# Modulation sums of the opening stage moved from VectorE to TensorE, with the last two blocks loaded singly

## Chip, cores and metric

The kernel runs on one core of a Trainium2 chip. The metric is device time in microseconds, the median of several runs.

## The reference, cut to what matters

One encoder layer on 2048 frames of width 1024. The conditioning vector `c` (1024 values) gives three vectors, and the first two modulate the input before the big projection:

```python
mod = c @ w_ada[l] + b_ada[l]                    # (1024) @ (1024 x 3072)
shift, scale, gate = jnp.split(mod, 3, axis=-1)
h = x * (1.0 + scale[:, None, :]) + shift[:, None, :]
proj = h @ w_in[l]                               # 1024 -> 3584, seven groups of 512
```

The seven groups of the projection feed a gated mixer and a stick-breaking attention; both results are multiplied by gates, projected out, scaled by `1 + gate`, added to the residual and normalised. All is float32. The kernel keeps that precision by splitting each operand of the big products into a rounded high part and a low remainder, and by summing three products (high by high, low by high, high by low).

## The kernel before, in words

The 2048 frames are four chunks of 512; the width of 1024 is eight blocks of 128. The kernel opens with chunk 3. For each of the eight blocks b it needs the shift and scale of these 128 columns (two columns of `w_ada`, 1024 rows each), the transposed input block, and the weights of the k and v groups (`w_in`). The output of a block is the modulated, transposed input in a high and a low half (`hts[b]`), and six accumulators in PSUM (`accs`: four of k, two of v) take three matmuls each from every block, 18 matmuls of 512 columns per block, 144 in all. This stage (lines 393 to 473) is called the opening here.

The order of TensorE, SyncE (which starts the loads), VectorE and ScalarE in the opening is the order in which the lines are written. A list `parts` (line 421) cuts the eight blocks into groups: 0; 1; 2 and 3; 4 and 5; 6 and 7. For each group:

- `load_ada` (line 283) loads the two slices of `w_ada`, for the shift and the scale, in tiles of 128 rows by partition; a group of one block takes two tiles with four DMAs, a group of two blocks four tiles with eight DMAs. Eight tiles of this kind exist, so a load waits for the release of an earlier group's tiles.
- `modulation` (line 296) multiplies on VectorE each of the eight row blocks by its part of `c` and adds it to `macc` (lines 302 and 304): eight instructions, over shift and scale together, 256 columns for one block and 512 for two.
- `modulation_sum` (line 307) sums `macc` over its 128 partitions on TensorE: for each block and each of shift and scale one float32 matmul with `macc` as the stationary operand and one column of ones as the moving one (line 312). Each such matmul is two instructions in the trace.
- `modulation_put` (line 316) adds `b_ada` and puts the sums into `mod_t` (line 319).
- `turn_x` (line 265) transposes a block of the input with four matmuls (line 268); `hidden` (line 271) applies the shift and scale on ScalarE (line 273); a ScalarE copy rounds that to the high half (line 454), and VectorE subtracts for the low half (line 461).
- `quarter` (line 116) loads raw weights of k and v for two blocks, into three buffers; `high` (line 416) rounds them on ScalarE, `low` (line 419) subtracts, on VectorE for k and on GpSimd for v.

`main(n)` issues n entries of the list `pending`, each the three matmuls of one block and one accumulator (line 160). After a group's transpose and sums comes `main(1)`; at the end of the group `main(len(pending))` issues what was left of the groups before, the new group's entries are appended, and `main(len(pending) - 6)` leaves the last block of them for the next group. So the products of block 0 stand behind the sums of block 1, the products of block 1 behind the sums of blocks 2 and 3, and so on. `advance` issues the VectorE steps of the next group's `modulation` between other VectorE work.

After the opening the results of k and v are stored, and the next stage (line 482 on) starts with the remaining products of chunk 3 and the modulation of chunk 2; its input loads (line 475) are queued on SyncE behind those of the opening.

Of the kernel before, what the change touches and what calls it, by code (L numbers as in the profile page):

```python
# [12 lines left out]
ALU = mybir.AluOpType  # L13
# [3 lines left out]
P = 128  # L17
D = 1024
S = 2048
NB = D // P  # L20
# [15 lines left out]
def layer_kernel(ctx: ExitStack, tc: tile.TileContext, x, c, w_ada, b_ada, w_in, ln_v_g, ln_v_b,  # L36
                 w_spatial, b_spatial, w_out, ln_g, ln_b, out):
    nc = tc.nc
# [40 lines left out]
    ones = const.tile([P, P], F32, name="ones")  # L79
# [26 lines left out]
    def pj(nm, shape=(P, 512)):  # L106
        return ps.tile(list(shape), F32, tag="pj", bufs=2, name=nm)

    def tr(nm, shape=(P, 512)):
        return ps.tile(list(shape), F32, tag="tr", bufs=3, name=nm)  # L110

    def zt(nm):
        return ps.tile([P, 2, CH], F32, tag="z", bufs=1, name=nm)


    def quarter(ws, g, b2, nm):

        raw = raw4(f"raw_{nm}_{b2}")
        nc.sync.dma_start(raw, w_in[b2 * 256:(b2 + 1) * 256, g * 512:(g + 1) * 512]
                          .rearrange("(b p) n -> p b n", p=P))  # L120
        sl = slice(2 * (b2 % 2), 2 * (b2 % 2) + 2)
        return raw, ws[b2 // 2][0][:, sl, :], ws[b2 // 2][1][:, sl, :]
# [27 lines left out]
    def mm3(acc, hts, ws, b, m, chan):  # L150

        sl = slice(m * P, (m + 1) * P)
        wh, wl = ws[b // 4][0][:, b % 4, :], ws[b // 4][1][:, b % 4, :]
        hh, hl = hts[b][:, 0, :], hts[b][:, 1, :]
        if chan:
            trip = ((wh[:, sl], hh), (wl[:, sl], hh), (wh[:, sl], hl))
        else:
            trip = ((hh[:, sl], wh), (hh[:, sl], wl), (hl[:, sl], wh))
        for i, (l_, r_) in enumerate(trip):
            nc.tensor.matmul(acc, l_, r_, start=(b == 0 and i == 0), stop=(b == NB - 1 and i == 2))  # L160
# [80 lines left out]
    with ExitStack() as sa:  # L241
        pa = sa.enter_context(tc.tile_pool(name="pa", bufs=1))

        def p2(nm, dt=F32):
            return pa.tile([P, CH], dt, tag="t2a", bufs=8, name=nm)
# [7 lines left out]
        c_t, bada_t = cb_t[:, 0:NB], cb_t[:, NB:3 * NB]  # L253
# [5 lines left out]
        def load_x(ci, b2):  # L259
            xt = pa.tile([P, 4, 256], F32, tag="xt", bufs=4, name=f"xt_{ci}_{b2}")  # L260
            nc.sync.dma_start(xt, x[ci * CH:(ci + 1) * CH, b2 * 256:(b2 + 1) * 256]
                              .rearrange("(t p) n -> p t n", p=P))
            return xt

        def turn_x(ci, b, xt):
            tp = tr(f"xT_{ci}_{b}")
            for t in range(4):
                nc.tensor.transpose(tp[:, t * P:(t + 1) * P], xt[:, t, (b % 2) * P:(b % 2 + 1) * P], ident)  # L268
            return tp
# [13 lines left out]
        def load_ada(b0, nb):  # L283

            rows = 4 // nb
            wts = []
            for r in range(NB // rows):
                wt = hta(f"wada_{b0}_{r}", (P, rows, 2, nb * P), F32)
                for i in range(2):
                    nc.sync.dma_start(wt[:, :, i, :], w_ada[r * rows * P:(r + 1) * rows * P,  # L290
                                                            i * D + b0 * P:i * D + (b0 + nb) * P]
                                      .rearrange("(b p) n -> p b n", p=P))
                wts += [wt[:, i] for i in range(rows)]
            return wts

        def modulation(b0, nb, wts):

            macc = p2(f"macc_{b0}")[:, 0:2 * nb * P].rearrange("p (two n) -> p two n", two=2)
            yield macc
            for b, wt in enumerate(wts):  # L300
                if b == 0:
                    nc.vector.tensor_scalar(macc, wt, c_t[:, b:b + 1], None, op0=ALU.mult)
                else:
                    nc.vector.scalar_tensor_tensor(macc, wt, c_t[:, b:b + 1], macc, op0=ALU.mult, op1=ALU.add)
                yield

        def modulation_sum(b0, nb, macc):

            mod_ps = ps.tile([P, 2 * nb], F32, tag="tr", bufs=3, name=f"mod_ps_{b0}")
            for i in range(2):  # L310
                for j in range(nb):
                    nc.tensor.matmul(mod_ps[:, i * nb + j:i * nb + j + 1], macc[:, i, j * P:(j + 1) * P],
                                     ones[:, 0:1], start=True, stop=True)
            return mod_ps

        def modulation_put(b0, nb, mod_ps):
            for i in range(2):
                cs = slice(i * NB + b0, i * NB + b0 + nb)
                nc.vector.scalar_tensor_tensor(mod_t[:, cs], mod_ps[:, i * nb:(i + 1) * nb], float(i), bada_t[:, cs],
                                               op0=ALU.add, op1=ALU.add)  # L320
# [74 lines left out]
        with tc.manual_schedule(engines={ET.PE, ET.SP, ET.DVE, ET.Activation}):  # L395
            zacc = zt("acc0")
            accs = [(pj("pk_0_0"), w_k, 0, True), (pj("pk_0_1"), w_k, 1, True), (tr("pk_0_2"), w_k, 2, True),
                    (ps.tile([P, 512], F32, tag="pv", bufs=1, name="pk_0_3"), w_k, 3, True),
                    (zacc[:, 0, :], w_v, 3, False), (zacc[:, 1, :], w_v, 2, False)]
            hts = []  # L400

            pending = []

            def main(n):
                for b, (acc, ws, m, chan) in pending[0:n]:
                    mm3(acc, hts, ws, b, m, chan)
                del pending[0:n]

            def advance(k=None):
                while k is None or k > 0:  # L410
                    if next(msteps, 0) == 0:
                        return
                    k = None if k is None else k - 1

            def high(raw, hi, lo):
                nc.scalar.copy(hi, raw)

            def low(raw, hi, lo, eng):
                eng.tensor_tensor(lo, raw, hi.bitcast(F32), op=ALU.subtract)

            parts = ((0, 1), (1, 1), (2, 2), (4, 2), (6, 2))
            xts = []
            wts = load_ada(*parts[0])
            xts.append(load_x(NC - 1, 0))
            rk = quarter(w_k, G_K, 0, "k")
            rv = None
            msteps = modulation(*parts[0], wts)
            macc = next(msteps)
            advance()
            for n, (b0, nb) in enumerate(parts):  # L430
                tps = [turn_x(NC - 1, b0, xts[b0 // 2])]
                mod_ps = modulation_sum(b0, nb, macc)
                main(1)
                fresh = b0 % 2 == 0
                rk0 = rk
                if n < len(parts) - 1:
                    b1, nb1 = parts[n + 1]
                    wts = load_ada(b1, nb1)
                    if n == 0:
                        rv = quarter(w_v, G_VB, 0, "v")  # L440
                    msteps = modulation(b1, nb1, wts)
                    macc = next(msteps)
                rv0 = rv
                if fresh:
                    high(*rk0)
                modulation_put(b0, nb, mod_ps)
                if nb == 2:
                    tps.append(turn_x(NC - 1, b0 + 1, xts[b0 // 2]))
                if fresh:
                    low(*rk0, nc.vector)  # L450
                hs = []
                for i in range(nb):
                    hs.append(hidden(NC - 1, b0 + i, tps[i]))
                    nc.scalar.copy(hs[i][1][:, 0, :], hs[i][0])
                if fresh:
                    high(*rv0)
                    low(*rv0, nc.gpsimd)
                advance(3)
                for i in range(nb):
                    hf, ht = hs[i]  # L460
                    nc.vector.tensor_tensor(ht[:, 1, :], hf, ht[:, 0, :].bitcast(F32), op=ALU.subtract)
                    hts.append(ht)
                    if i < nb - 1:
                        advance(1)
                if n < len(parts) - 1 and b1 % 2 == 0:
                    xts.append(load_x(NC - 1, b1 // 2))
                    rk = quarter(w_k, G_K, b1 // 2, "k")
                    rv = quarter(w_v, G_VB, b1 // 2, "v")
                advance()
                main(len(pending))  # L470
                pending += [(b, a) for b in range(b0, b0 + nb) for a in accs]
                main(len(pending) - 6)
            main(len(pending))
        with tc.manual_schedule(engines={ET.PE, ET.SP, ET.DVE, ET.Activation}):
            xnext = [load_x(NC - 2, b2) for b2 in range(NB // 2)]
# [440 lines left out]
    n = len(units)  # L916
# [4 lines left out]
    with tc.manual_schedule(engines={ET.PE}):  # L921
        for i in range(n + 3):
# [7 lines left out]
            f = load[i] * rate[phase[0]] * scale / 3 if i else 6000  # L930
# [42 lines left out]
```

## Time and profile before

| | us |
|---|---|
| median of 3 runs | 1317.86 (1316.92 to 1319.66) |
| the profiled execution | 1317.15 |
| its span | 1315.0 |
| TensorE busy | 1246.9 (95%) |
| VectorE busy | 950.8 (72%) |
| ScalarE busy | 556.3 (42%) |
| GpSimd busy | 212.4 (16%) |
| mean granted TensorE clock | 0.987 |

A row of the timeline has the start in microseconds from the span's start, the time that its instructions took, the engine (PE is TensorE's matmul, PEld its weight load, DVE VectorE, ACT ScalarE, POOL GpSimd, SPq the queue of SyncE), the line, the operation, output and inputs, and how many instructions were merged. In brackets stands the idle time before it and what ended it. Starts of consecutive matmuls tell their pace; the durations of matmuls overlap. A row of the windows gives busy microseconds and instruction counts by engine, the granted clock (1.00 is 2.4 GHz, 0.50 is 1.2 GHz), the mean busy share of the DMA engines and GB/s.

### The profile page before, as it was taken

To read this page: it belongs to the slowest core of one execution; us is meant where nothing else is said; L and a number is where in the kernel's file an instruction comes from. 1 tells how busy PE (TensorE), PEld (TensorE's weight loads), DVE (VectorE), ACT (ScalarE), POOL (GpSimd) and SP (SyncE) were. 2 spreads that over 40 slices of the span, in tenths; PEclk is the share of its full clock that TensorE was granted. 3 is DMA by queue.
4 is the path that set the end of the run, shared out by engine and by line. 5 is a ranking of instruction groups with operands and counts; after the bars stand their busy time and mean duration, and the time that the engine had idled before them with its cause. 6 is when DMAs were issued, how large, how long until landed. Compare 5 with 4: busy or idle time off the path is not lost.

```text
span 1315.0 us, 18685 instructions
## 1 busy us (share of the span) xinstructions
PE 1246.9 (95%) x6678; PEld 1055.5 (80%) x6678; DVE 950.8 (72%) x1358; ACT 556.3 (42%) x1063; POOL 212.4 (16%) x342
## 2 busy tenths in 40 slices
PE   4999999899889999899979999999999999999997
PEld 4788877688678888787868888888888888888875
DVE  6634453317678778888888887878788798888874
ACT  3333222214434454555555554545444444444430
POOL 1244333001110002233260000000000011010001
PEclk9999999899899999999989999999999999999999
DMA  9699886858789874674546483745759776754431
GB/s 318 202 365 326 281 276 198 280 176 263 254 267 312 245 224 144 207 226 141 156 115 188 114 252 98 236 111 158 213 174 282 224 207 161 201 167 149 128 101 48
DMA packets 202012, 269.20 MB, mean 205 GB/s; under 512 B 14880, under 2 KB 131648, under 8 KB 200896
## 3 DMA queue, kind: packets, MB, share of 16 engines
q1 hardware_dynamic: 191280, 234.41, 58.8%
q0 software_dynamic: 10592, 33.59, 7.5%
q8 instruction: 53, 0.87, 0.3%
q14 instruction: 39, 0.32, 0.1%
q10 hardware_dynamic: 48, 0.01, 0.0%
HBM read 180.37 MB, written 83.36 MB: 201 GB/s over the span
## 4 chain that ended last, share of the span: by engine, by line
PE 72%; issue 8%; DVE 8%; DMA 5%; POOL 3%; ACT 1%; SPq 1%; POOLq 0%; DVEq 0%; ACTq 0%
PE puz_False L160 13%; PE po L671 12%; PE pkv L160 11%; PE pqz_True L160 8%; PE tr L808 7%; PE pv L827 4%; PE z L778 4%; PE z L779 4%; PE pv L825 4%; PE pva_False L160 3%; DVE kp L793 2%; DMA wada<-in_w_ada_dram 2%; DMA qt<-q_d 1%; DVE wtl L68 1%; PE xT L268 1%
## 5 line engine op out<-in xcount | busy, mean ns | idle before, releaser
L793 DVE TENSOR_TENSOR_SCAN kp<-kp,kp,zero 128x512 f32<-128x512 f32 x192 | 241.5, 1286 | 48.8 <-ACT kp L782 48.6
L65 ACT CAST wth<-tr 128x512 fp32r<-128x512 f32 (+2 forms) x352 | 169.9, 487 | 249.0 <-PE tr L808 149.3
L68 DVE TENSOR_TENSOR wtl<-tr,wth 128x512 fp32r<-128x512 f32 (+2 forms) x352 | 194.1, 561 | 31.1 <-ACT wth L65 28.3
L671 PE MATMUL po<-wo,mt 128*128 128x512 f32 x744 | 201.9, 403 | 0.1
L782 ACT ACTIVATE kp<-z 128x128 f32<-128x128 f32 (+3 forms) x224 | 147.8, 691 | 101.6 <-PE z L779 99.9
L808 PE MATMUL tr<-ident,kp 128*128 128x128 f32 x1088 | 168.4, 275 | 6.6 <-DVE wtl L68 3.6
L785 POOL TENSOR_SCALAR_AFFINE_SELECT kp<-kp 128x128 f32<-128x128 f32 x128 | 56.5, 450 | 678.4 <-ACT kp L782 572.1
L671 PEld LDWEIGHTS po<-wo,mt 128*128 128x128 f32 x744 | 132.6, 188 | 24.2 <-DVE xr L681 0.5
L808 PEld LDWEIGHTS tr<-ident,kp 128*128 128x128 f32 x1088 | 128.4, 141 | 24.4 <-DVE wtl L68 3.4
L825 PE MATMUL pv<-wth,vs 128*128 128x256 f32 x576 | 143.1, 279 | 2.3 <-DVE ot L841 2.1
L827 PE MATMUL pv<-wtl,vs 128*128 128x256 f32 x576 | 142.4, 285 | 2.0 <-DVE wtl L68 2.0
L793 DVE TENSOR_TENSOR_SCAN kp<-kp,zero 128x128 f32<-128x128 f32 (+3 forms) x128 | 107.7, 865 | 34.6 <-POOL kp L785 32.0
L778 PE MATMUL z<-ks,qt 128*128 128x512 f32 (+2 forms) x320 | 115.7, 367 | 5.0 <-DMA qt<-q_d 4.3
L825 PEld LDWEIGHTS pv<-wth,vs 128*128 128x128 f32 x576 | 110.9, 193 | 11.0 <-DVE ot L841 4.3
L827 PEld LDWEIGHTS pv<-wtl,vs 128*128 128x128 f32 x576 | 110.9, 193 | 8.8 <-DVE wtl L68 2.4
L779 PE MATMUL z<-ks,qt 128*128 128x512 f32 (+2 forms) x320 | 116.7, 365 | 0.0
L160 PE MATMUL pkv<-wh_v,hta 128*128 128x512 f32 x224 | 75.8, 402 | 0.5 <-DVE el_k L68 0.5
L160 PE MATMUL pqz_True<-ht_qz,wh_q 128*128 128x512 f32 x192 | 70.0, 411 | 5.7 <-DMA ht_qz<-ht_d 5.7
L160 PE MATMUL puz_False<-wh_u,ht_uz 128*128 128x512 f32 x192 | 73.5, 411 | 1.7 <-DMA ht_uz<-ht_d 1.7
L778 PEld LDWEIGHTS z<-ks,qt 128*128 128x128 f32 x320 | 60.2, 188 | 17.6 <-ACT woh L65 4.7
L160 PE MATMUL pva_False<-wh_va,ht_va 128*128 128x512 f32 x192 | 71.8, 411 | 1.0 <-DMA ht_va<-ht_d 1.0
L160 PE MATMUL puz_False<-wh_za,ht_uz 128*128 128x512 f32 x192 | 72.6, 411 | 0.0
(191 smaller groups left out, 2234.5 us busy)
## 6 DMA issues: line engine op xcount, KB each, us to landing
ks<-k_d SPq DMA_DIRECT2D x160, 128.0 KB, 3.9
vs<-v_d SPq DMA_DIRECT2D x80, 256.0 KB, 3.6
qt<-q_d SPq DMA_DIRECT2D x64, 256.0 KB, 5.0
ht_d<-hta POOLq DMA_DIRECT2D x24, 512.0 KB, 5.8
ht_qz<-ht_d SPq DMA_DIRECT2D x24, 512.0 KB, 7.1
ht_va<-ht_d SPq DMA_DIRECT2D x24, 512.0 KB, 6.1
ht_uz<-ht_d SPq DMA_DIRECT2D x24, 512.0 KB, 5.9
wada<-in_w_ada_dram SPq DMA_DIRECT2D x32, 256.0 KB, 6.6
```

The source lines that it names most:

```text
L65: nc.scalar.copy(hi, src)
L68: (sub or nc.vector).tensor_tensor(lo, src, hi.bitcast(F32), op=ALU.subtract)
L160: nc.tensor.matmul(acc, l_, r_, start=(b == 0 and i == 0), stop=(b == NB - 1 and i == 2))
L671: nc.tensor.matmul(acc, ms[l_], w[:, r_, :], start=(b == 0 and i == 0), stop=(b == NB - 1 and i == 2))
L778: nc.tensor.matmul(z[:, j, 0:w_], hd.q[:, 0, qs], hd.k[self.s][:, 0:w_], start=True, stop=False)
L779: nc.tensor.matmul(z[:, j, 0:w_], hd.q[:, 1, qs], hd.k[self.s][:, 0:w_], start=False, stop=True)
L782: nc.scalar.activation(self.kp[:, js, 0:w_], z[:, js, 0:w_], AF.Sigmoid, scale=-ZSC)
L785: nc.gpsimd.affine_select(own, own, pattern=[[-1, P]], compare_op=ALU.is_gt, fill=1.0, base=0, channel_multiplier=1)
L793: nc.vector.tensor_tensor_scan(kp[:, j, 0:w_][:, ::-1], kp[:, j, 0:w_][:, ::-1], zero.broadcast_to([P, w_]), 1.0 if self.diag else self.pr ...
L808: nc.tensor.transpose(tp[:, e, j * P:(j + 1) * P], self.kp[:, j, kb * P:(kb + 1) * P], ident)
L825: nc.tensor.matmul(self.pv[:, cs], hd.v[self.s][:, kb, :], self.wt[0][:, kb, cs], start=self.diag and kb == 0, stop=False)
L827: nc.tensor.matmul(self.pv[:, cs], hd.v[self.s][:, kb, :], self.wt[1][:, kb, cs], start=False, stop=self.s == 0 and kb == self.nkb - 1)
```

## The change

The list of groups becomes 0; 1; 2 and 3; 4 and 5; 6; 7. For a group of one block (0, 1, 6, 7) VectorE does no modulation at all: TensorE sums shift and scale directly, with each of the eight 128 by 128 pieces of `w_ada` as the stationary operand and one column of `c` as the moving one, eight accumulating matmuls for each sum. For a group of two blocks VectorE sums only the scale (256 columns instead of 512), TensorE sums the shift directly. The low part of the v weights moves from GpSimd to VectorE, behind the low halves of the group. The products of block 0 and of block 1 are issued at the end of their own group, ahead of the next group's transpose and sums.

```diff
         def modulation(b0, nb, wts):
-            macc = p2(f"macc_{b0}")[:, 0:2 * nb * P].rearrange("p (two n) -> p two n", two=2)
+            if nb == 1:
+                yield None
+                return
+            macc = p2(f"macc_{b0}")[:, 0:nb * P]
             yield macc
             for b, wt in enumerate(wts):
                 if b == 0:
-                    nc.vector.tensor_scalar(macc, wt, c_t[:, b:b + 1], None, op0=ALU.mult)
+                    nc.vector.tensor_scalar(macc, wt[:, 1], c_t[:, b:b + 1], None, op0=ALU.mult)
                 else:
-                    nc.vector.scalar_tensor_tensor(macc, wt, c_t[:, b:b + 1], macc, op0=ALU.mult, op1=ALU.add)
+                    nc.vector.scalar_tensor_tensor(macc, wt[:, 1], c_t[:, b:b + 1], macc, op0=ALU.mult, op1=ALU.add)
                 yield
 
-        def modulation_sum(b0, nb, macc):
+        def modulation_sum(b0, nb, macc, wts):
             mod_ps = ps.tile([P, 2 * nb], F32, tag="tr", bufs=3, name=f"mod_ps_{b0}")
             for i in range(2):
                 for j in range(nb):
-                    nc.tensor.matmul(mod_ps[:, i * nb + j:i * nb + j + 1], macc[:, i, j * P:(j + 1) * P],
-                                     ones[:, 0:1], start=True, stop=True)
+                    col, cs = mod_ps[:, i * nb + j:i * nb + j + 1], slice(j * P, (j + 1) * P)
+                    if i and macc is not None:
+                        nc.tensor.matmul(col, macc[:, cs], ones[:, 0:1], start=True, stop=True)
+                        continue
+                    for b, wt in enumerate(wts):
+                        nc.tensor.matmul(col, wt[:, i, cs], c_t[:, b:b + 1], start=b == 0, stop=b == NB - 1)
             return mod_ps
...
-            parts = ((0, 1), (1, 1), (2, 2), (4, 2), (6, 2))
+            parts = ((0, 1), (1, 1), (2, 2), (4, 2), (6, 1), (7, 1))
...
-                mod_ps = modulation_sum(b0, nb, macc)
+                mod_ps = modulation_sum(b0, nb, macc, wts)
...
                 if fresh:
                     high(*rv0)
-                    low(*rv0, nc.gpsimd)
                 advance(3)
...
+                if fresh:
+                    low(*rv0, nc.vector)
                 if n < len(parts) - 1 and b1 % 2 == 0:
                     xts.append(load_x(NC - 1, b1 // 2))
...
                 pending += [(b, a) for b in range(b0, b0 + nb) for a in accs]
-                main(len(pending) - 6)
+                main(len(pending) - (6 if n > 1 else 0))
             main(len(pending))
```

## Rows read from the trace of the kernel before

**Rows 1.** Windows of ten microseconds: PE, PEld, DVE, ACT, POOL busy, clock, DMA share, GB/s

```profile
10.00:20.00 10.00, 2.62 (x13) 2.22 (x12) 7.58 (x12) 3.39 (x4) 2.38 (x1) 1.00 1.12 336
20.00:30.00 10.00, 10.00 (x43) 8.26 (x44) 7.94 (x15) 3.64 (x5) 0.00 (x0) 1.00 1.09 359
30.00:40.00 10.00, 8.61 (x45) 7.10 (x44) 8.70 (x10) 3.52 (x5) 2.73 (x1) 1.00 1.09 359
40.00:50.00 10.00, 9.27 (x45) 7.46 (x44) 9.74 (x13) 4.71 (x6) 2.73 (x1) 1.00 1.01 329
...
60.00:70.00 10.00, 10.00 (x50) 8.30 (x49) 3.26 (x6) 4.36 (x8) 5.38 (x10) 1.00 0.48 170
```

**Rows 2.** Timeline of TensorE, start to the first products

```profile
9.49 1.11 PE L268 MATMUL xT<-ident,xt 128*128 128x128 f32 x4 [5.16 <-DMA xt<-in_x_dram]
10.40 0.85 PE L312 MATMUL mod_ps<-ones,macc 128*128 128x1 f32 x4
11.11 1.09 PE L268 MATMUL xT<-ident,xt 128*128 128x128 f32 x4
19.59 1.01 PE L312 MATMUL mod_ps<-ones,macc 128*128 128x1 f32 x4 [7.38 <-DVE macc L304]
20.46 0.77 PE L160 MATMUL pk<-hta,wh_k 128*128 128x512 f32 x1
...
21.46 1.05 PE L160 MATMUL pk<-hta,wh_k 128*128 128x512 f32 x2
22.31 0.63 PE L160 MATMUL pk<-hta,wl_k 128*128 128x512 f32 x1
```

**Rows 3.** Timeline of TensorE, from the third group's sums to the opening's end

```profile
26.95 0.60 PE L268 MATMUL xT<-ident,xt 128*128 128x128 f32 x4
27.39 1.02 PE L312 MATMUL mod_ps<-ones,macc 128*128 128x1 f32 x8
28.28 0.48 PE L160 MATMUL pk<-hta,wh_k 128*128 128x512 f32 x1
...
37.04 0.60 PE L268 MATMUL xT<-ident,xt 128*128 128x128 f32 x4
39.02 1.02 PE L312 MATMUL mod_ps<-ones,macc 128*128 128x1 f32 x8 [1.39 <-DVE macc L304]
...
48.67 0.60 PE L268 MATMUL xT<-ident,xt 128*128 128x128 f32 x4
50.66 1.02 PE L312 MATMUL mod_ps<-ones,macc 128*128 128x1 f32 x8 [1.39 <-DVE macc L304]
51.55 0.49 PE L160 MATMUL pk<-hta,wh_k 128*128 128x512 f32 x1
...
61.91 0.39 PE L160 MATMUL pk<-hta,wh_k 128*128 128x512 f32 x1
...
65.99 0.39 PE L160 MATMUL pkv<-wh_v,hta 128*128 128x512 f32 x1
```

**Rows 4.** Timeline of ScalarE and VectorE behind the second and third groups' sums

```profile
20.95 0.78 ACT L273 ACTIVATE hf<-xT,mod_t 128x512 f32<-128x512 f32 x1 [4.16 <-DVE mod_t L319]
21.76 0.62 ACT L454 CAST hta<-hf 128x512 fp32r<-128x512 f32 x1
...
13.11 0.35 DVE L302 TENSOR_SCALAR macc<-wada,cb_t 128x256 f32<-128x256 f32 x1
13.49 1.01 DVE L304 SCALAR_TENSOR_TENSOR macc<-wada,cb_t,macc 128x256 f32<-128x256 f32 x2
...
28.59 1.22 DVE L419 TENSOR_TENSOR wl_k<-raw_k,wh_k 128x1024 fp32r<-128x1024 f32 x1
29.73 0.48 DVE L302 TENSOR_SCALAR macc<-wada,cb_t 128x512 f32<-128x512 f32 x1
30.24 1.54 DVE L304 SCALAR_TENSOR_TENSOR macc<-wada,cb_t,macc 128x512 f32<-128x512 f32 x2
31.70 0.69 DVE L461 TENSOR_TENSOR hta<-hf,hta 128x512 fp32r<-128x512 f32 x1
```

**Rows 5.** Timeline of GpSimd and VectorE at one of the moved subtractions

```profile
32.57 2.73 POOL L419 TENSOR_TENSOR wl_v<-raw_v,wh_v 128x1024 fp32r<-128x1024 f32 x1 [13.32 <-ACT wh_v L416]
...
32.96 2.89 DVE L461 TENSOR_TENSOR hta<-hf,hta 128x512 fp32r<-128x512 f32 x1
```

**Rows 6.** Windows of one microsecond: the granted clock and the DMA share

```profile
49.00:50.00 1.00, 0.27 (x3) 0.03 (x1) 0.96 (x2) 0.00 (x0) 0.00 (x0) 1.00 0.43 139
...
52.00:53.00 1.00, 1.00 (x8) 0.86 (x7) 1.00 (x1) 0.92 (x2) 0.00 (x0) 0.82 0.00 0
...
56.00:57.00 1.00, 1.00 (x6) 0.82 (x5) 0.00 (x0) 0.00 (x0) 1.00 (x1) 0.97 0.07 23
```

**Rows 7.** DMA issues: size and microseconds from issue to landing

```profile
wada<-in_w_ada_dram SPq DMA_DIRECT2D x32, 256.0 KB, 6.6
```

## The prediction

> **What bounds the kernel now.** I read the windows first, to see which engine is full in the opening, then the timeline of TensorE, then those of the engines that feed it. From 20 to 66 us TensorE is all but full: 10.00, 8.61 and 9.27 us busy in three windows of ten, and full again from 60 us on, when the next stage begins [rows 1]. The DMA engines are as full as it is up to 49.5 us [rows 1, 6], but nothing in TensorE's rows after 9.49 us waits for a transfer [rows 2, 3]. What is idle on TensorE is listed quickly: from the end of the second transpose at 12.20 to 19.59, a wait for VectorE's `macc`, and twice 1.39 us, for the same reason, at 39.02 and 50.66 [rows 2, 3]. The last product of the opening ends where the next stage's first begins, at 65.99 [rows 3]. Behind that TensorE stays full, so I pass a delay of this point on to the end of the kernel one for one. So the question is: how much work does TensorE get, how much of it fits into these waits of 7.4 and 2.8 us, and what new waits arise.
>
> **What is added.** Before, the sums are 4, 4, 8, 8, 8 = 32 instructions. After, a single block takes 2 x 8 matmuls of two instructions each, 32; a pair takes 16 matmuls for the shift and 2 for the scale, 36. In all 32 + 32 + 36 + 36 + 32 + 32 = 200, so 168 more, although each moves one column. Their pace is in the rows: eight from 27.39 to 28.28, 0.111 us each [rows 3]. At the lower clock four take 0.71 or 0.87 us, 0.18 to 0.22 each [rows 2]; I take 0.20. That the new ones accumulate in one column is no reason for a slower pace, since the two instructions of one matmul do that already. So 168 x 0.111 = 18.6 us of work come to an engine with 10.2 us of idle time, and most of that idle time cannot be used, because sums have to precede the hidden block that products need.
>
> **What is removed.** VectorE loses the 128x256 steps of both first blocks, the 512-wide steps of the last pair, and a third of the rest: three steps for a pair cost 0.35 + 1.01 = 1.36 instead of 0.48 + 1.54 = 2.02 us [rows 4]. The four v subtractions that move to VectorE, at some 1.22 each [rows 4], are less than that. They take away the stretch in which GpSimd's 2.73 us subtraction held a 0.69 us VectorE instruction for 2.89 us [rows 4, 5]. All this is off the path now: what VectorE made late was only the 10.2 us above.
>
> **New waits.** Block 0's and block 1's products move ahead of the next sums. This brings them forward, but nothing stands between a block's sums and its products any more. The chain is in the rows behind the second group's sums: they end at 20.60, the hidden block starts on ScalarE at 20.95 and its high half ends at 22.38, so 1.8 us; the low half takes 0.69 more, of which two products from the high half hide 0.45, so 2.1 at the full clock [rows 2, 4]. For the first pair VectorE has the 1.22 us k subtraction and three modulation steps in front: the low half ended at 32.39, 4.0 after the sums' end at 28.41, and will come 0.66 earlier, at 3.3; less 0.45 hidden, about 3.0 [rows 3, 4]. Later groups have a previous block's products to cover this.
>
> **The path, at a clock that holds once it has risen.** A product block of 18 matmuls takes 61.91 to 65.99, 4.08 us [rows 3], and at the lower clock 18 x 0.425 = 7.7 [rows 2]; a transpose 0.44 or, low, 0.91 [rows 2, 3]. Transpose 0 starts at 9.49 as now, its input being loaded in the same place of the queue. Sums 0: 10.40 + 32 x 0.20 = 16.8. Wait 1.8: 18.6. Products 0 at the lower clock: 26.3. Transpose and sums 1 (0.44 + 3.55): 30.3. Wait 2.1 and products 1: 36.5. Transpose and sums 2 (0.44 + 36 x 0.111): 40.9. Wait 3.0 and products 2: 48.0. Transpose and sums of blocks 4 and 5: 52.4. Transpose 5, products 3 and 4: 61.0. Transpose and sums 6, products 5: 69.1. Transpose and sums 7: 73.1. Products 6 and 7: 81.3. Against 65.99 that is 15.3 us more.
>
> **Queues.** On SyncE the second half of the pair's `w_ada` for blocks 4 and 5 waits for block 1's tiles, now released by sums 1 at 30.3 instead of by VectorE at 19.6; four issues and 6.6 us to land [rows 7] make about 41, ahead of sums at 48.4. Behind it stand the input and weights of these blocks. The v weights of blocks 6 and 7 wait for the k subtraction after sums 4 and 5, about 54, and block 7's `w_ada` is queued behind them: 54 + 4 issues + 6.6 is about 64, sums 7 start at 69.5. Their cover is 5 us; if it went, its excess would be added before products 6. The next stage's input follows, the last of it behind transpose 7, and is needed by the second half of that stage. I cost these at nothing. Splitting the last pair into two loads moves the same bytes, and transfers, done by 49.5 now, are no longer what ends last. The moved v subtraction delays its first reader by at most some tenths, since four k accumulators come first.
>
> **The clock.** It fell once in the opening. The window of 52 to 53 shows 0.82, so 0.36 us of it at half, a fall at 52.64; that of 56 to 57 shows 0.97, a rise at 56.06: 3.4 us at 1.2 GHz, 1.7 us lost [rows 6]. Ahead of it stand a wait of 1.39, eight sums of 0.89 us, three products and a transpose [rows 3]. The same wait and sums at 37.64 to 39.91 did not bring a fall, but there products stood right ahead [rows 3]. So one short run of narrow sums beside a wait already stands at the edge, and the change makes five runs of 3.6 to 4.0 us, three of them with waits of 2 to 3 us beside them. My estimate is one such stretch for each of sums 1 to 5, 5 x 1.7 = 8.5 us. Bounds: none, or two stretches each, 17 us. The Trainium skill (TensorE: Matmul & The Clock Gate, Why this matters for your kernels) puts a fall down to gaps in which TensorE does nothing; by that rule the narrow sums, being work, would hold the clock. This speaks for the sum without the 8.5 us, and the fall at 52.64, behind an idle time no longer than the one that was harmless, speaks against it.
>
> **Sum.** The profiled execution took 1317.15 us, 0.7 below the median. 1317.15 + 15.3 + 8.5 = 1341.
>
> **Rivals.**
> - The narrow sums hold the clock: 1317.15 + 15.3 = 1332.4, and if sums 0 also raise it before products 0, 3.6 less, 1328.9. For it: TensorE is working. Against it: the fall at 52.64.
> - The clock falls twice for each of these sums, or the chain to the products is longer: 1317.15 + 15.3 + 17 = 1349.5 and above.
> - Faster, by one mechanism: long runs of single-column matmuls go at a smaller step than the eight in a row do. Of the 81.3 us the sums are 6.4 + 18.6 = 25.0; they would have to shrink to 9.7, a step of 0.043 instead of 0.111, to come out even. At 0.025 they are 5.6 us, the end moves to 61.9, and the time is 1313. Against it stand three runs of eight, all at 0.111 [rows 3]. The Trainium skill's table of issue gaps (same page, Back-to-back issue gap) gives about 25 ns for so few columns, without the weight load; the rows, with a load for each, do not agree.
> - That nothing happens (the cover is as good as now) needs a step between 0.03 and 0.055; the written order leaves no other way.
>
> **Chances.** Clock falls about once for each of the sums: 0.55. Clock held: 0.29. Worse than two falls each: 0.06. Faster: 0.06. No change: 0.04. A difference within 0.2%, 2.6 us, is about what a measurement of this kernel cannot tell from none. The range goes from the held clock with an early rise to two falls each, 1329 to 1350.
>
> **What would show it.** In the changed kernel's timeline: 32 sums from about 10.4 to 17, first products at 18 to 19 instead of 20.46, runs of 32 or 36 sums of 3.6 to 4.0 us (7 at the lower clock), waits of 2 to 3 us for ScalarE's and VectorE's halves ahead of products 0, 1 and 2, and the next stage starting near 90 instead of 65.99, near 81 if the clock holds. The windows should show granted clocks of 0.50 behind runs of sums. Wrong would be: sums at a step well under 0.1, first products before 16, a TensorE wait for `wada` or raw weights, or a later stage that makes the delay good.

## The result and the profile after

The changed kernel takes 1338.98 us (median of 4 runs, 1335.86 to 1340.78) against 1318.12 before: a ratio of 1.0155 with a 95% interval of 1.013 to 1.018, slower. The forecast was 1341. The profiled execution has a span of 1338.5 us, 23.5 above the 1315.0 of before, and nearly all of that arises in the opening. TensorE's timeline of the changed kernel, cut to transposes, sums (line 320, and line 317 where `macc` is left), the first products of a block and the start of the next stage:

```profile
9.34 1.12 PE L268 MATMUL xT<-ident,xt 128*128 128x128 f32 x4 [4.87 <-DMA xt<-in_x_dram]
10.24 6.83 PE L320 MATMUL mod_ps<-cb_t,wada 128*128 128x1 f32 x32
18.91 0.80 PE L160 MATMUL pk<-hta,wh_k 128*128 128x512 f32 x1 [1.84 <-ACT hta L461]
...
24.76 0.60 PE L268 MATMUL xT<-ident,xt 128*128 128x128 f32 x4
25.20 3.63 PE L320 MATMUL mod_ps<-cb_t,wada 128*128 128x1 f32 x32
30.66 0.79 PE L160 MATMUL pk<-hta,wh_k 128*128 128x512 f32 x1 [1.83 <-ACT hta L461]
...
37.39 0.60 PE L268 MATMUL xT<-ident,xt 128*128 128x128 f32 x4
37.83 3.63 PE L320 MATMUL mod_ps<-cb_t,wada 128*128 128x1 f32 x32
41.32 0.59 PE L317 MATMUL mod_ps<-ones,macc 128*128 128x1 f32 x4
42.32 0.63 PE L268 MATMUL xT<-ident,xt 128*128 128x128 f32 x4 [0.41 <-DVE mod_t L326]
43.74 0.80 PE L160 MATMUL pk<-hta,wh_k 128*128 128x512 f32 x1 [0.80 <-ACT hta L461]
...
51.53 3.63 PE L320 MATMUL mod_ps<-cb_t,wada 128*128 128x1 f32 x32
...
66.25 3.63 PE L320 MATMUL mod_ps<-cb_t,wada 128*128 128x1 f32 x32
...
76.00 3.63 PE L320 MATMUL mod_ps<-cb_t,wada 128*128 128x1 f32 x32
...
89.41 0.39 PE L160 MATMUL pkv<-wh_v,hta 128*128 128x512 f32 x1
```

The next stage starts at 89.41 instead of 65.99 [rows 3], 23.4 us later; behind it the kernel takes 1249.1 us, as it did before (1315.0 - 65.99 = 1249.0). The products of block 0 come at 18.91 instead of 20.46 [rows 2], the only products that are earlier. Every run of 32 sums takes 3.5 us from its start to the next instruction's (51.53 to 55.02), 0.109 each, and the first one at the lower clock 6.8. Ahead of three product blocks stand waits for ScalarE's high half.

The granted clock of the same kernel, in those windows of one microsecond in which it falls or rises again (columns as in rows 1):

```profile
29.00:30.00 1.00, 0.00 (x0) 0.00 (x0) 0.93 (x5) 0.79 (x2) 0.00 (x0) 0.63 0.67 203
...
36.00:37.00 1.00, 1.00 (x6) 0.83 (x5) 0.00 (x0) 0.00 (x0) 0.00 (x0) 0.96 0.44 169
...
42.00:43.00 1.00, 0.63 (x4) 0.42 (x4) 1.00 (x3) 0.73 (x1) 0.00 (x0) 0.95 0.00 0
...
49.00:50.00 1.00, 1.00 (x5) 0.77 (x4) 0.30 (x1) 0.00 (x0) 0.00 (x0) 0.63 1.23 295
...
56.00:57.00 1.00, 1.00 (x7) 0.89 (x6) 1.00 (x1) 0.97 (x2) 0.00 (x0) 0.78 0.09 16
...
59.00:60.00 1.00, 1.00 (x4) 0.81 (x3) 0.75 (x2) 1.00 (x2) 0.00 (x0) 0.51 0.97 370
...
70.00:71.00 1.00, 1.00 (x4) 0.77 (x4) 1.00 (x3) 0.76 (x1) 0.00 (x0) 0.61 0.00 0
...
73.00:74.00 1.00, 1.00 (x5) 0.83 (x4) 0.87 (x1) 0.00 (x0) 0.00 (x0) 0.69 0.02 8
...
80.00:81.00 1.00, 1.00 (x5) 0.75 (x4) 0.00 (x0) 0.97 (x2) 0.00 (x0) 0.73 0.00 0
...
83.00:84.00 1.00, 1.00 (x4) 0.75 (x3) 0.00 (x0) 0.00 (x0) 0.00 (x0) 0.57 0.00 0
```

Read in pairs, a fall and the rise after it, they are the stretches at 1.2 GHz: five, one behind each of sums 1 to 5. The shares give their ends: from 29.26 to 36.08, 42.90 to 49.74, 56.56 to 59.98, 70.22 to 73.62 and 80.46 to 83.86, 23.9 us in all. Before there was one [rows 6].

Up to TensorE's first rise, at about 22 us here and 25 us before, this column shows 1.00, although TensorE goes at half the pace: a sum takes 0.213 us and a product 0.43, as in the stretches at 0.50. Where the first 25 us are said to be at the lower clock, that is read from this pace, and the stretches at half clock that are counted below leave it out.

### The profile page after: what moved, and what is told of

It reads as the page before. It is cut to its first block, busy times and chain, and to the rows that moved or that the text cites. A ratio compares the mean times of both kernels' runs of the same rounds, so it can differ in the third digit from the quotient of the medians.

```text
span 1338.5 us, 18997 instructions
## 1 busy us (share of the span) xinstructions
PE 1277.9 (95%) x6846; PEld 1085.4 (81%) x6846; DVE 932.5 (70%) x1340; ACT 556.4 (42%) x1063; POOL 202.6 (15%) x338
## 4 chain that ended last, share of the span: by engine, by line
PE 74%; issue 9%; DVE 7%; DMA 6%; POOL 2%; ACT 1%; SPq 0%; POOLq 0%; DVEq 0%; ACTq 0%
PE puz_False L160 12%; PE pkv L160 11%; PE po L679 11%; PE tr L816 7%; PE pqz_True L160 6%; PE pva_False L160 4%; PE pv L835 4%; PE pv L833 4%; PE z L787 4%; PE z L786 4%; PE pk L160 2%; PE mod_ps L320 2%; DVE kp L801 2%; DMA ht_va<-ht_d 1%; DMA ht_uz<-ht_d 1%
## 5 line engine op out<-in xcount | busy, mean ns | idle before, releaser
L816 PEld LDWEIGHTS tr<-ident,kp 128*128 128x128 f32 x1088 | 129.0, 141 | 23.9 <-DVE wtl L68 3.8
```

The costliest lines, as they stand in the source:

```text
L816: nc.tensor.transpose(tp[:, e, j * P:(j + 1) * P], self.kp[:, j, kb * P:(kb + 1) * P], ident)
```

## The experiments

The question is which of three things costs how much: the added work of TensorE, the waits that the new order of the products makes, and the clock; and what lowers the clock, the narrowness of the sums or the waits beside them. Where a kernel's opening ends (the start of line 160's first instruction of the next stage) is read from its profiled execution; medians and ratios are against runs of the kernel before on the same chip.

| kernel | next stage starts at, us | granted clock at half in the opening, us | median, us | ratio to before (95%) |
|---|---|---|---|---|
| before | 65.99 | 3.4 | 1318.12 | |
| the change | 89.41 | 23.9 | 1338.98 | 1.0155 (1.0130 to 1.0180) |
| the change, again | 89.73 | 23.9 | 1337.59 | 1.0158 (1.0131 to 1.0184) |
| products of block 1 one group behind | 87.15 | 23.9 | 1340.52 | 1.0169 (1.0139 to 1.0199) |
| sums of 128 columns | 79.74 | 3.4 | 1334.39 | 1.0117 (1.0083 to 1.0151) |
| the same, again | 81.76 | 6.8 | 1332.31 | 1.0118 (1.0094 to 1.0143) |
| both of these | 73.58 | 0 | 1326.84 | 1.0063 (1.0041 to 1.0085) |
| all sums on VectorE | 66.77 | 6.8 | 1320.62 | 1.0024 (1.0007 to 1.0041) |
| the same, products all one behind | 66.77 | 3.4 | 1318.20 | 1.0007 (0.9992 to 1.0022) |
| before, v subtraction on VectorE | 62.67 | 0 | 1315.84 | 0.9976 (0.9957 to 0.9994) |
| the same, again | 62.63 | 0 | 1315.64 | 0.9986 (0.9966 to 1.0006) |
| the same, and block 1's sums on TensorE | 60.25 | 3.4 | 1316.36 | 0.9985 (0.9968 to 1.0002) |

**The waits or the narrow sums.** In the first kernel block 1's products stay behind the pair's sums, so that TensorE does not wait for them:

```diff
-                main(len(pending) - (6 if n > 1 else 0))
+                main(len(pending) - (6 if n > 0 else 0))
```

> The changed kernel, but the products of block 1 stay one group behind, as before the change, so that they cover the chain behind the pair's sums. The sums stay as narrow as they are, TensorE's waits of 1.8 and 2.0 us ahead of products 1 and 2 go. Theory 1 (runs of single-column sums lower the clock by themselves): the clock still falls behind each run, four or five times, and the time is about 1333 us, the waits being saved and no more. Theory 2 (the waits beside the sums lower it): the falls behind sums 1 and 2 go too, and the time is below 1329 us.

Measured: 1340.52 us, a miss for both theories, and telling. Two rows of its timeline of TensorE and two windows of its clock:

```profile
28.94 0.66 PE L268 MATMUL xT<-ident,xt 128*128 128x128 f32 x4 [0.32 <-DVE mod_t L326]
29.81 6.99 PE L320 MATMUL mod_ps<-cb_t,wada 128*128 128x1 f32 x32 [0.21 <-ACT hf L273]
```

```profile
29.00:30.00 1.00, 0.79 (x5) 0.55 (x6) 0.93 (x3) 0.97 (x2) 0.00 (x0) 0.74 0.67 224
...
43.00:44.00 1.00, 1.00 (x5) 0.79 (x5) 1.00 (x2) 0.35 (x1) 0.00 (x0) 0.93 1.19 319
```

The waits ahead of products 1 and 2 are gone (0.32 and 0.21 us are left) and the clock falls all the same, at the same place and for longer: with sums 1 and sums 2 side by side it stays at 1.2 GHz from 29.48 to 43.14, and sums 2 take 6.99 us instead of 3.63. In all the opening has 23.9 us at half clock, as many as with the waits, though in three stretches instead of five. So waits of this length are not needed for a fall. That the time did not drop to 1333 has two reasons. The end of the opening moved by 2.3 us only: 2.8 us of waits went and the first input came 0.6 us earlier, but TensorE's busy time from the first transpose on grew from 74.89 to 76.04 us, since less of the half clock fell into waits. And behind the opening this execution took 1251.2 us, 2.1 more than the changed kernel's.

The second kernel keeps order and waits, and makes the sums wide: `cw` holds each value of `c` in 128 equal columns, and only the first column of the result is used.

```diff
-                        nc.tensor.matmul(col, wt[:, i, cs], c_t[:, b:b + 1], start=b == 0, stop=b == NB - 1)
+                        nc.tensor.matmul(col, wt[:, i, cs], cw[:, b, :], start=b == 0, stop=b == NB - 1)
```

> The changed kernel with the same number of sums, but each moves 128 equal columns instead of one (VectorE makes the columns once, in eight instructions at the start) and the result is read from the first. The order, the waits and the count of instructions stay. Theory 1 (few moved columns are what lowers the clock): if the step stays near 0.111 us, as it is for the transposes, which move 128 columns, the clock rises during sums 0 and does not fall behind the others, five stretches at half clock go (8 to 9 us), sums 0 take some 5 instead of 6.8 us, and the time is 1325 to 1331 us. Theory 2 (the waits lower it): falls as in the changed kernel, 1337 to 1341 us. If a float32 matmul of 128 columns takes longer than its weight load, up to 0.22 us, up to 19 us come on top in either case, and the granted clock decides.

Measured: 1334.39 us, above the range I gave for theory 1, though the opening did what theory 1 said. Its TensorE timeline, cut to sums and waits, and its clock:

```profile
10.47 5.57 PE L323 MATMUL mod_ps<-cw,wada 128*128 128x128 f32 x32
17.88 0.50 PE L160 MATMUL pk<-hta,wh_k 128*128 128x512 f32 x1 [1.84 <-ACT hta L464]
...
22.81 3.74 PE L323 MATMUL mod_ps<-cw,wada 128*128 128x128 f32 x32
28.38 0.50 PE L160 MATMUL pk<-hta,wh_k 128*128 128x512 f32 x1 [1.84 <-ACT hta L464]
...
79.74 0.39 PE L160 MATMUL pkv<-wh_v,hta 128*128 128x512 f32 x1
```

```profile
41.00:42.00 1.00, 1.00 (x4) 0.82 (x5) 1.00 (x3) 1.00 (x2) 0.00 (x0) 0.80 0.88 299
...
45.00:46.00 1.00, 1.00 (x5) 0.80 (x5) 0.00 (x0) 0.00 (x0) 0.00 (x0) 0.99 1.17 304
```

A run of 32 takes 3.74 us instead of 3.63, so 127 more columns per instruction cost next to nothing. The waits ahead of products 0 and 1 are the same 1.84 us. But TensorE's pace rises during sums 0 (5.57 us instead of 6.83) and the granted clock falls once instead of five times, and the next stage starts 9.7 us earlier. The clearest comparison is the part from the transpose of block 4 to the next stage, in which neither kernel has a wait. The changed kernel first, then the wide sums:

```profile
51.09:89.41 38.32, 38.32 (x208) 33.21 (x207) 10.75 (x18) 10.68 (x15) 2.31 (x4) 0.87 0.39 122
46.24:79.74 33.50, 33.50 (x208) 29.68 (x206) 10.74 (x18) 10.70 (x15) 2.30 (x4) 1.00 0.46 144
```

TensorE is busy all the time in both, with the same number of matmuls; the narrow sums bring three falls there, the wide ones none, and that is 4.8 us. So it is the narrow sums that lower the clock in this part, and no wait takes part in it. In this part three executions with narrow sums (the change twice, and with block 1's products one behind) show three, three and two falls, three with wide sums show none. Waits have a share elsewhere: the one fall that is left comes behind waits of 0.41, 0.80 and 0.78 us ahead of products 2, and the kernels below with the sums on VectorE fall beside waits of 1.45 and 2.40 us. Not every such wait brings a fall: that of 1.84 us ahead of products 0 brought none here and one, at 18.96, in the repeat.

As 9.7 us in the opening became 4.6 in the median, both kernels ran again, on one chip.

> The changed kernel itself, unaltered, for a comparison on one chip with the wide sums: 1336 to 1341 us, five falls of the granted clock in the opening, next stage from about 89 us.

> The changed kernel with sums that move 128 equal columns, once more. If the width of the sums alone decides the clock, the opening shows at most one or two falls, its end lies 7 to 10 us ahead of the changed kernel's, and the median over twelve runs is 5 to 10 us below that of the changed kernel on the same chip. If the gain of the first time was one of phase, the two medians differ by less than 3 us.

Measured: 1337.59 and 1332.31 us, from five runs each instead of twelve (1337.48 to 1339.85 and 1331.69 to 1335.97). The opening ends 8.0 us earlier (81.76 against 89.73), with two falls, and the medians differ by 5.3. That is inside the range, at its lower end. In the profiled executions the rest of the kernel took 1245.8 us behind the narrow sums this time and 1250.2 behind the wide ones; it differs by several us from execution to execution, as the clock does: the windows of one microsecond behind the opening have 38.3 us at half clock in the first and 48.9 in the second. So the opening's gain is shown, and that all of it reaches the end is not.

**What is left without clock and waits.** Both edits together:

> The changed kernel with sums of 128 columns and with the products of block 1 one group behind, so that neither the clock nor the waits ahead of products 1 and 2 are left of the loss; what stays is the added work of TensorE. If the long stretch at half clock of the kernel with narrow sums and the same order came from the narrow sums, it is gone here, the next stage begins at 75 to 78 us and the time is 1326 to 1330 us. If it came from the order, the clock falls here too, and the next stage begins at 79 us or later.

Measured: 1326.84 us, no fall at all in the opening, no TensorE wait above 0.4 us behind the first products, next stage at 73.58, a little better than expected. Two of its rows:

```profile
27.01 3.84 PE L323 MATMUL mod_ps<-cw,wada 128*128 128x128 f32 x32 [0.20 <-ACT hf L276]
...
73.58 0.39 PE L160 MATMUL pkv<-wh_v,hta 128*128 128x512 f32 x1
```

The sums that took 6.99 us in the same place take 3.84. So the long fall came from the width, not from the order. Taken off in this sequence, the opening's 23.4 us are in three parts: 89.41 - 79.74 = 9.7 for the narrow sums' effect on the clock, the earlier rise during sums 0 included; 79.74 - 73.58 = 6.2 for the order of the products with its waits, one fall included and some 0.8 us of a still earlier rise; 73.58 - 65.99 = 7.6 for TensorE's added work, as far as its idle time of before did not take it. The split between the first two depends on the sequence: with the order taken off first it is 2.3 for the order (89.41 - 87.15) and 13.6 for the clock (87.15 - 73.58).

**The other parts of the change.** All sums go back to VectorE (both functions as before, with the unused argument), the rest of the change stays:

> The changed kernel with all sums back on VectorE; the order of the products, the split of the last pair and the moved v subtraction stay. If the 168 added TensorE instructions and what they do to the clock are the whole loss, the time comes back to that of before or below it: products of block 0 run from about 15 us, VectorE's steps pace the pairs at some 11 us, the next stage begins at 62 to 66 us, and the time is 1313 to 1319 us. If the order of the products or the split cost something of their own (new waits of 2 to 3 us behind three of the sums, nothing to cover them), it is 1322 us or more.

Measured: 1320.62 us, between the two cases, 0.24% above before. Three rows of TensorE:

```profile
12.58 0.80 PE L160 MATMUL pk<-hta,wh_k 128*128 128x512 f32 x1 [2.05 <-ACT hta L454]
...
33.38 1.22 PE L160 MATMUL pk<-hta,wh_k 128*128 128x512 f32 x2 [1.45 <-DVE hta L460]
...
58.02 0.58 PE L312 MATMUL mod_ps<-ones,macc 128*128 128x1 f32 x4 [2.40 <-DVE macc L304]
...
66.77 0.39 PE L160 MATMUL pkv<-wh_v,hta 128*128 128x512 f32 x1
```

Block 0's products start 8 us earlier than before, and all of this is lost again: VectorE paces the groups, TensorE waits for the halves of the pair, the clock falls at that wait for 6.8 us, and 2.40 us go by for the sums of block 7. So the sums are 1338.98 - 1320.62 = 18 us of the loss, and order and split a few.

The moved subtraction by itself, in the kernel before:

```diff
                     high(*rv0)
-                    low(*rv0, nc.gpsimd)
...
+                if fresh:
+                    low(*rv0, nc.vector)
```

> The kernel before with one part of the change alone: the low part of the v weights on VectorE, behind the low halves, instead of on GpSimd. If the stretches in which a VectorE instruction of 0.7 us took 2.4 to 2.9 beside GpSimd's are on the path (VectorE's sums are what TensorE waits for), the second sums come 1.9 us earlier and each later group about 1 us, and the time is 1313 to 1316.5 us. If not, it is within 0.2% of before.

> The kernel before with the v subtraction on VectorE, once more, on another day's chip: 0.2 to 0.3% below before (1313 to 1316 us) if the first result holds, within 0.1% of before if it was one of phase.

Measured: 1315.84 and 1315.64 us, ratios of 0.9976 and 0.9986. The first lies in its range, the second, 0.14% below before, between its two cases. Both runs are listed for chip 6, 23 minutes apart, so the second is a repeat and not another chip. In the opening this part is a gain of its own. VectorE's low half, and TensorE's sums behind it, in the first of these runs:

```profile
32.13 0.68 DVE L460 TENSOR_TENSOR hta<-hf,hta 128x512 fp32r<-128x512 f32 x1
...
33.40 0.68 DVE L460 TENSOR_TENSOR hta<-hf,hta 128x512 fp32r<-128x512 f32 x1
```

```profile
38.39 1.02 PE L312 MATMUL mod_ps<-ones,macc 128*128 128x1 f32 x8 [0.32 <-DVE macc L304]
...
48.96 1.02 PE L312 MATMUL mod_ps<-ones,macc 128*128 128x1 f32 x8 [0.32 <-DVE macc L304]
...
62.67 0.39 PE L160 MATMUL pkv<-wh_v,hta 128*128 128x512 f32 x1
```

The half that took 2.89 us beside GpSimd [rows 5] takes 0.68, the groups follow each other in 10.57 us instead of 11.64, and the opening ends 3.3 us earlier. The Trainium skill (SBUF - State Buffer, Who interferes with whom) says that a VectorE instruction with two inputs in SBUF and a GpSimd one that reads SBUF share a port, and that the later one waits until the other is through. The rows agree: 32.57 + 2.73 is 35.30, and the blocked instruction ended at 35.85, 0.55 behind, about its own 0.68 [rows 5]. The second sums, which I expected 1.9 us earlier, come at 20.02, 0.43 later than before: VectorE's remaining steps for them now stand behind the subtraction, and that waits 1.82 us for ScalarE's high part of the v weights. In the whole kernel the gain is at the limit of what was measured: one interval ends below 1, the other at 1.0006.

With the split added:

> All sums on VectorE, the v subtraction on VectorE, the last pair split into two single blocks, but the order of the products as before the change (one block behind). Against the kernel with only the subtraction moved this adds the split alone. If the split is what the kernel with all sums on VectorE lost, VectorE's steps for block 7 make TensorE wait about 2.3 us ahead of the last sums and the next stage begins at 64 to 65 us: 1317 to 1320 us. If the order is, the next stage begins at 62 to 63 us and the time is 1314 to 1316.5 us.

Measured: 1318.20 us, in the range of the case for the split, though the next stage begins at 66.77, 2 us later than that case had it. TensorE waits for block 7's sums as expected, and the clock falls once behind that wait, 3.4 us at half:

```profile
56.41 0.58 PE L312 MATMUL mod_ps<-ones,macc 128*128 128x1 f32 x4 [2.40 <-DVE macc L304]
```

Against the kernel with the subtraction alone moved, the opening ends 4.1 us later (66.77 against 62.67), about the wait of 2.40 and half of the 3.4, and the ratio rises by 0.2 to 0.3%. So the split costs some 4 us. That the order of the products costs something of its own while the sums are on VectorE is not shown: with either order the next stage begins at 66.77, and the intervals of the two ratios, 1.0024 and 1.0007, overlap.

A version that uses the idle stretch alone: the v subtraction on VectorE, and block 1's sums, 128 columns wide, on TensorE.

> The kernel before with the v subtraction on VectorE, and with the sums of block 1 alone on TensorE (32 instructions of 128 columns), where TensorE had 8.5 us of nothing to do. If VectorE is what paced the second sums, these end at about 17 us instead of 21, VectorE begins the pair's steps 2 to 3 us earlier, the next stage begins at 59 to 61 us and the time is 1311 to 1314.5 us, below both kernels. If the transfers of the pair's w_ada (the DMA engines are full up to 49 us) arrive no earlier than the steps needed them, it is that of the kernel with the subtraction alone moved, 1314 to 1317 us.

Measured: 1316.36 us, ratio 0.9985 with an interval that holds 1. The opening ends at 60.25, as the first case expected, the earliest of all, but the time lies in the range of the second: no more of that reaches the end than of the subtraction alone. Its new wait is a transfer:

```profile
11.63 5.29 PE L316 MATMUL mod_ps<-cw,wada 128*128 128x128 f32 x32
...
23.04 0.63 PE L269 MATMUL xT<-ident,xt 128*128 128x128 f32 x4 [2.01 <-DMA xt<-in_x_dram]
...
60.25 0.39 PE L160 MATMUL pkv<-wh_v,hta 128*128 128x512 f32 x1
```

Why did an opening that is 5.7 us shorter than that of before not show as 5 us in the median? In its profiled execution the rest took 1255.3 us, 6.3 more than before. The windows of the rest, before and then this kernel:

```profile
65.99:1315.00 1249.01, 1200.29 (x6470) 1017.02 (x6468) 906.76 (x1288) 533.62 (x1033) 199.17 (x329) 0.99 0.66 202
60.25:1315.50 1255.25, 1206.96 (x6470) 1023.27 (x6468) 906.29 (x1288) 534.36 (x1033) 200.42 (x329) 0.98 0.65 201
```

TensorE is idle for as long in both, 48.7 and 48.3 us; the same 6470 matmuls keep it busy 6.7 us longer. In windows of one microsecond it stands at half clock for 32.5 us of the rest of before and for 53.6 here (51.7 and 52.6 in the two runs with the subtraction alone moved). So in these executions the gain of the opening was lost to the clock in later stages, not to new waits. Why the clock falls more there stays open, and one profile of each is not enough to call it an effect of the change: other executions of before have mean granted clocks from 0.980 to 0.987, and the profiled one has 0.987.

## Why the prediction was right

- **What bounds it.** TensorE, from 20 us on: right. With 168 narrow sums taken back (all sums on VectorE) 18 us came back; with them on TensorE, 128 columns wide and block 1's products one group behind, 7.6 us of delay stayed in the opening.
- **The pace of the sums.** 0.111 us at the full clock and 0.20 at the lower one were forecast; runs of 32 took 3.5 and 6.8 us, 0.109 and 0.213. The eight sums that stood in the trace of before were enough to price 200. The rival with a step of 0.025 us fell.
- **The waits.** 1.8 us ahead of products 0: measured 1.84. 2.1 ahead of products 1: 1.83, and the low half cost nothing beyond it, since the products ran at the lower clock. About 3.0 ahead of products 2 with the transpose in it was too much: it was 1.83, from the sums' end at 41.91 to 43.74, and 0.30 more for the low half. The low half came 3.3 us behind the sums, as forecast, but the two products ahead of it ran at the lower clock and hid 1.2 us instead of 0.45.
- **The path.** Point by point, forecast (with 1.7 us for each fall that had come by then) and measured: first products 18.6 and 18.91; second transpose 26.3 and 24.76, because the clock rose during products 0 and not behind them; third transpose 38.2 and 37.39; transpose of block 4 51.4 and 51.09; of block 6 66.1 and 65.81; of block 7 75.9 and 75.56; next stage 89.8 and 89.41. Two errors cancel here, and that is luck: products 0 took 5.85 us instead of 7.7, 1.9 less, and the two falls that lasted twice as long as the one of before made products 1 and 2 take 6.73 and, without the wait of 0.30, 7.05 instead of 4.08 + 1.7 each, 2.2 more.
- **The clock.** One fall for each of sums 1 to 5 was forecast and five came. Three lasted 3.4 us, two 6.8. The wide sums show that this was the right mechanism: with them the opening ends at 79.74. The sum without falls, 81.3, less 3.6 for a rise before products 0, plus 1.7 for the one fall that is left, is 79.4. What speaks for it in the trace of before was thin, one fall behind eight sums and a wait of 1.39 us, where a wait of the same length with products ahead of it did no harm. The Trainium skill's rule (TensorE: Matmul & The Clock Gate, Why this matters for your kernels), gaps without work, misses this: in the kernel with block 1's products one behind, the clock fell with waits of 0.32 and 0.21 us, and in the changed kernel it fell three times in 38.32 us without a wait.
- **Queues.** `w_ada`, inputs and raw weights were on time: behind the first transpose TensorE waits for no transfer, as before.
- **Passing it on.** In the profiled executions one for one held for the change (23.4 us in the opening, 23.5 in the span), in part by chance: behind the opening TensorE had 32.5 us at half clock before and 41.8 after, and idle times of 48.7 and 46.4 us. The medians are 20.9 us apart, and 20.2 in the repeat. In the other direction it did not hold: openings that end 3.3 and 5.7 us earlier gave 1 to 2 us in the median.

## What to carry to other kernels

Before work moves to an engine, ask in which stage that engine is full; TensorE's idle share over the whole stage says little when the sums must come ahead of what it waits for. A matmul instruction of one column took 0.109 to 0.111 us here, as good as one of 128 columns at 0.112, and runs of 32 of them also cost the clock of the products behind them; with 128 equal columns the clock held, except at some of the waits. An order that brings products forward is worth little if it takes away the cover of the next chain. And a shorter opening has to be checked at the end of the kernel: here later falls of the clock took most of it.

## What I had not expected

- Making the moving operand 128 times as wide made the kernel faster: 3.74 instead of 3.63 us for 32 sums, and an opening that ends 8.0 to 9.7 us earlier.
- Two runs of narrow sums side by side put TensorE at 1.2 GHz for 13.7 us without any wait above 0.4 us, and slowed the second run itself to 0.214 us a sum.
- Four subtractions that moved from GpSimd to VectorE, the engine with more to do, shortened the opening by 3.3 us.
